# Second MLP's up projection: seven block products in place of eight

## The chip, the cores and the metric

One core of one Trainium2 chip runs one program. The metric is the device time of one execution in microseconds, the median over runs; before the change three runs gave 2939.75 us (2938.02 to 2944.45).

## What is computed

One inference step of a two-layer decoder trunk for 1024 prompt tokens and 64 sample tokens, 1088 rows in all, of width 1024. Layer 0 mixes with RWKV-7 and gated DeltaNet heads, layer 1 with an RG-LRU; each layer is followed by a squared-ReLU MLP of inner width 4096, and a final norm ends it. What the change touches is the end of layer 1:

```python
yc, hl, cl = lru_mix(xn, w_in_odd[i], lru_conv_w[i], lru_conv_b[i], ...)
h = h + yc @ w_out_odd[i]
h = h + sq_relu_mlp(rmsnorm(h, norm_mlp[l]), mlp_up[l], mlp_down[l])
y = rmsnorm(h, norm_final)

def sq_relu_mlp(x, up, down):
    return jnp.square(jax.nn.relu(x @ up)) @ down
```

## The kernel before

Activations lie transposed: `h[f]`, f = 0 to 7, is feature tile f, 128 features on the partitions and 1088 tokens along the row. Tokens come in two halves (`HALVES`): columns 0 to 575 in two chunks of 288 and columns 576 to 1087 in one chunk of 512 (`CH`). A chunk's accumulator is one PSUM bank; `dense` takes it in turn from the pools psd and psc, two banks each, so four accumulators are open at most. A third pool, psa, has two banks more.

Every large matrix product is made of three terms in float32r: an operand x is split into hi = round(x) and lo = x - hi, the weights likewise, and `dense` adds wh·xh, wh·xl and wl·xh over the tiles k of the contraction. `wraw` loads raw weights into tiles "wraw" (128 x 512, 256 KB a DMA, from SyncE's queue, SP), `wsplit` makes "whi" on ScalarE and "wlo" on VectorE. There are four raw buffers and four hi/lo pairs. `split` does the same for activations.

`lru` ends with `gate(7)`, whose product is stored to a DRAM tensor "yl", and with `rows_out`, which transposes final states and stores them from POOL's queue. `outproj` loads yl in tiles "mid" (six buffers of 576), splits them into x tiles, and adds to h the eight feature tiles of the projection, first those of half 0, then those of half 1.

`mlp(1, h)` norms h (`norm_half`: operands are split with the norm's weight, and the factor 1/rms, "rs", is applied to the product) and then runs eight blocks. In a block the up projection makes four feature tiles of the middle: 8 weight tiles x 3 terms for each of the three chunks, `relu2` takes each from PSUM, and its square is split into two "big" tiles (hi and lo; twelve buffers). The down projection then adds the block's share to all eight h[f]: 4 tiles x 3 terms for each chunk. The last block takes the chunks in turn, so that `final` can start on rows that are done.

Tile framework and engines: a scheduler puts the program's operations into one fixed order for each engine ahead of the run; each engine and each DMA queue works in that order, and what waits holds up what is behind it. A tile that reuses memory waits for the last reader of what lay there.

```python
for blk in range(8):
    for j in range(4):
        w = self.wload(up[:, :, f * P:(f + 1) * P], 8, P)
        mh, ml = self.big(F32R), self.big(F32R)
        for c0, n in chs:
            self.relu2(m, self.dense(w, 0, P, xs, c0, n), c0, n)
            self.split((mh[:, c0:c0 + n], ml[:, c0:c0 + n]), m)
```

Of the kernel before, what the change touches and what calls it, by code (L numbers as in the profile page):

```python
# [100 lines left out]
class Kern:  # L101
# [336 lines left out]
    def mlp(self, l, h, xs=None, early=0):  # L438
# [5 lines left out]
        for blk in range(8):  # L444
            mids = []
            for j in range(4):
                f = blk * 4 + j
                w = self.wload(up[:, :, f * P:(f + 1) * P], 8, P)
                mh, ml = self.big(F32R), self.big(F32R)
                chs = CH  # L450
                if f < early:
                    chs = CH[2:]
                    m = self.mid(TA)
                    nc.sync.dma_start(m, self.ma[:, f, :])
                    self.split((mh[:, :TA], ml[:, :TA]), m)
# [6 lines left out]
            passes = [(CH, ())] if blk < 7 or l == 0 else [  # L462
                (CH[:2], ()), (((TA, 256),), (0, 1, 2, 3, 8)), (((TA + 256, 256),), (4, 5)), ((), (6, 7))]
            if len(passes) > 1:
                self.final_weights()
            for chs, done in passes:
                done = list(done)
                for fo in range(4 if chs else 0):
                    w = self.wload(down[:, blk * 4:(blk + 1) * 4, fo * 256:(fo + 1) * 256], 4, 256)
                    for s in range(2):  # L470
                        f = fo * 2 + s
                        for c0, n in chs:
                            ps = self.dense(w, s * P, P, mids, c0, n)
                            self.tt(h[f][:, c0:c0 + n], h[f][:, c0:c0 + n], ps, ALU.add)
                        if f and done:
                            self.final(h, done.pop(0))
                for t in done:
                    self.final(h, t)


    def outproj(self, w_out, xs, ys, h):

        w_out = w_out.rearrange("(k p) f -> p k f", p=P)
        for hf, (c0, n, _) in enumerate(HALVES):
            for k, x in enumerate(xs):
                y = self.mid(n)
                self.nc.sync.dma_start(y[:, :512], ys[:, k, hf * 512:hf * 512 + 512])
                if hf == 0:
                    self.nc.sync.dma_start(y[:, 512:], ys[:, k, NP:])
                self.split(x[hf], y)  # L490
        for c0, n, chs in HALVES:
            for f in range(8):
                w = self.wload(w_out[:, :, f * P:(f + 1) * P], 8, P)
                for cc, m in chs:
                    ps = self.dense(w, 0, P, xs, cc, m)
                    self.tt(h[f][:, cc:cc + m], h[f][:, cc:cc + m], ps, ALU.add)


    def evac(self, pp, psx, pre, ps, c0, n, b0=0, end=NP, rs=None):
# [1118 lines left out]
def body(tc, a, o, stop=None, dbg=None):  # L1618
    with ExitStack() as es:
# [1 line left out]
        K.setup()  # L1621
        K.even()
        K.wpools(es, 4 - WBUF[0], 4 - WBUF[1])
        K.xp = K.pool(es, "xp")
        K.wk = K.pool(es, "wk")
        hp = K.pool(es, "h0")
        h = [hp.tile([P, T], F32, name=f"h{f}") for f in range(8)]
        K.dp = (K.psd, K.psc)
        for _ in K.ahead(*AHEAD[1:]):
            pass  # L1630
# [39 lines left out]
```

## Time and profile before

| what | value |
|---|---|
| runs | 2939.75 us median, 2938.02 to 2944.45 |
| the profiled execution | 2938.02 us, of it a span of 2935.6 us from first to last instruction |
| TensorE (PE) | 2843.6 us busy, 20284 matmuls |
| VectorE (DVE), ScalarE (ACT) | 1580.4 and 1131.5 us busy |
| mean granted TensorE clock | 0.984 |
| odd output projection | 2058.9 to 2155.6 us from the span's start |
| second MLP, from its first up matmul | from 2156.7 us |

Times in rows are microseconds from the span's start, unless marked ns. PE's matmuls are pipelined and their ends are modelled, so a row's duration overlaps the next row; what one costs in a stream is the distance from start to start. A wait is idle time of an engine in front of an instruction, with what ended it. An engine that waits while it is not the bottleneck costs nothing. A row of busy time by stretch holds start and end, length, then busy time and count of PE, of PE's weight loads, of DVE, ACT and POOL, then the granted clock (1.00 is 2.4 GHz), the DMA engines' busy share and the GB/s they moved.

### The profile page before, as it was taken

The page shows a single profiled execution, that of the slowest core. Times are in us where ns is not written, and L with a number is a line of the kernel's source. Part 1 is how long each engine was busy: PE and PEld are TensorE (multiplying, and loading weights), DVE is VectorE, ACT ScalarE, POOL GpSimd, SP SyncE. Part 2 cuts the span into 40 slices and gives each one's busy share as a digit, 9 for nine tenths or more (in the row PEclk, how much of TensorE's full clock was granted, in tenths as well). Part 3 has the DMA queues.
Part 4 walks back from the last instruction along what each step waited for, and adds up shares of the span by engine and source line. Part 5 has one row for each costly group of instructions (what it writes and reads, how often), then busy time and mean ns, then how long its engine had stood idle before and what let it go on. Part 6 is the DMA issues. An engine that isn't in the chain of part 4 may idle for free. (4 is left out here: it accounts for less than half of the span.)

```text
span 2935.6 us, 50667 instructions
## 1 busy us (share of the span) xinstructions
PE 2843.6 (97%) x20284; PEld 2503.9 (85%) x20284; DVE 1580.4 (54%) x3390; ACT 1131.5 (39%) x2289; POOL 126.3 (4%) x337
## 2 busy tenths in 40 slices
PE   7999998989998999999999999999999999999998
PEld 6997776667887898988889999888989999999998
DVE  4365776678747662644443336677643333333335
ACT  6455444335445432522222224656441222112224
POOL 2111001110000000000000000000000000000000
PEclk9999999799998999999999999999999999999999
DMA  5345444335344345522222111121421111111113
GB/s 187 112 120 149 115 105 106 93 98 138 108 126 125 101 139 156 176 74 81 74 78 58 44 46 44 46 67 63 150 65 44 44 44 50 44 44 44 44 58 126
DMA packets 421842, 263.21 MB, mean 90 GB/s; under 512 B 95333, under 2 KB 393119, under 8 KB 421606
## 3 DMA queue, kind: packets, MB, share of 16 engines
q1 hardware_dynamic: 415478, 243.99, 29.0%
q0 software_dynamic: 5696, 14.86, 1.6%
q8 instruction: 159, 2.61, 0.4%
q10 hardware_dynamic: 432, 1.11, 0.1%
q14 instruction: 77, 0.63, 0.1%
HBM read 206.17 MB, written 53.73 MB: 89 GB/s over the span
## 5 line engine op out<-in xcount | busy, mean ns | idle before, releaser
L157 PE MATMUL m<-xh,whi 128*128 128x288 f32 (+3 forms) x2984 | 991.3, 333 | 4.9 <-DVE big L151 1.4
L157 PE MATMUL m<-xl,whi 128*128 128x288 f32 (+3 forms) x2984 | 987.7, 331 | 0.2 <-DVE xl L151 0.2
L157 PE MATMUL m<-xh,wlo 128*128 128x288 f32 (+3 forms) x2984 | 980.4, 329 | 0.2 <-DVE wlo L151 0.2
L148 ACT ACTIVATE whi<-wraw 128x512 fp32r<-128x512 f32 x533 | 334.1, 629 | 1050.2 <-PE m L157 970.8
L157 PE MATMUL m<-big,whi 128*128 128x288 f32 (+2 forms) x3136 | 727.3, 323 | 0.0
L157 PEld LDWEIGHTS m<-xh,whi 128*128 128x128 f32 (+1 forms) x2984 | 561.6, 189 | 54.5 <-DVE big L151 2.0
L157 PEld LDWEIGHTS m<-xh,wlo 128*128 128x128 f32 (+1 forms) x2984 | 562.2, 189 | 42.8 <-issue 1.0
L157 PEld LDWEIGHTS m<-xl,whi 128*128 128x128 f32 (+1 forms) x2984 | 562.1, 188 | 42.6 <-issue 2.0
L157 PEld LDWEIGHTS m<-big,whi 128*128 128x128 f32 x3136 | 527.9, 188 | 38.1
L151 DVE TENSOR_TENSOR wlo<-wraw,whi 128x512 fp32r<-128x512 f32 x533 | 364.7, 686 | 325.3 <-ACT whi L148 316.7
L157 PE MATMUL m<-big,wlo 128*128 128x288 f32 (+2 forms) x1568 | 506.5, 323 | 0.0
L151 DVE TENSOR_TENSOR h<-h,m 128x288 f32<-128x288 f32 (+2 forms) x416 | 217.8, 524 | 353.1 <-PE m L157 353.1
L157 PEld LDWEIGHTS m<-big,wlo 128*128 128x128 f32 x1568 | 294.3, 188 | 19.4
L148 ACT ACTIVATE mid<-mid 128x288 f32<-128x288 f32 (+1 forms) x202 | 104.2, 518 | 238.9 <-DVE mid L154 203.2
L154 DVE SCALAR_TENSOR_TENSOR mid<-m,rs 128x512 f32<-128x512 f32 (+1 forms) x154 | 85.4, 554 | 176.6 <-PE m L157 176.6
L151 DVE TENSOR_TENSOR big<-mid,big 128x288 fp32r<-128x288 f32 (+2 forms) x170 | 99.4, 585 | 120.8 <-ACT big L148 120.4
L148 ACT ACTIVATE big<-mid 128x288 fp32r<-128x288 f32 (+2 forms) x170 | 92.6, 545 | 7.0 <-DMA mid<-ma 2.1
L154 DVE SCALAR_TENSOR_TENSOR fpo<-fpp,vt,fpo 128x512 f32<-128x512 f32 x100 | 74.5, 745 | 29.2 <-ACT fpo L148 24.9
L148 ACT ACT_TABLE_LOAD x62 | 79.5, 1283 | 9.4 <-PE m L157 6.3
L148 ACT ACTIVATE fpp<-m 128x288 f32<-128x288 f32 (+1 forms) x78 | 35.0, 449 | 56.2 <-PE m L157 47.8
L151 DVE TENSOR_TENSOR tbtmp<-lb,tb 32x15 f32<-32x15 f32 (+8 forms) x270 | 51.5, 191 | 6.3 <-DMA lb<-rs 2.0
L151 DVE TENSOR_TENSOR tb<-tb,tbtmp 32x15 f32<-32x15 f32 (+8 forms) x270 | 52.0, 193 | 4.6
(386 smaller groups left out, 2580.2 us busy)
## 6 DMA issues: line engine op xcount, KB each, us to landing
wraw<-mlp_up SPq DMA_DIRECT2D x172, 256.0 KB
wraw<-mlp_down SPq DMA_DIRECT2D x144, 256.0 KB
wraw<-w_in_even SPq DMA_DIRECT2D x120, 256.0 KB
wraw<-w_out_even SPq DMA_DIRECT2D x32, 256.0 KB
wraw<-w_in_odd SPq DMA_DIRECT2D x32, 256.0 KB
wraw<-w_out_odd SPq DMA_DIRECT2D x32, 256.0 KB
in<-rd SPq DMA_DIRECT2D x8, 896.0 KB
mid<-ma SPq DMA_DIRECT2D x22, 288.0 KB
```

Source lines behind the costliest of these rows:

```text
L148: return self.nc.scalar.activation(out, in_, f, **kw)
L151: return self.nc.vector.tensor_tensor(out, a, b, op)
L154: return self.nc.vector.scalar_tensor_tensor(out, a, s, b, op0, op1, **kw)
L157: return self.nc.tensor.matmul(out, l, r, start=start, stop=stop, **kw)
```

## The change

The up projection of the second MLP is made by Strassen's scheme (Winograd's form). A pair j of feature tiles (2j, 2j+1), the two halves of the contraction (h[0..3] and h[4..7]) and a pair of token chunks (288 and 288, or 256 and 256) give 2 x 2 blocks, and the four block results come from seven block products in place of eight. Each product adds over four tiles k. Its operands are sums of blocks: of weights, made for each pair ("s1", "s2" and one raw tile overwritten), and of the normed h ("T1" to "T4", and three plain blocks), made once and kept for all 16 pairs in new pools (xq: 2 x 28 operands as hi and lo). The 512 chunk of half 1 is now a pair of 256. Three banks a pair of chunks (A, B, C) hold the products; B takes three in turn, read out between by DVE into temporaries "t1", "u2", "u3".

The operands are computed while the output projection runs. Its loads from yl now go through four buffers "tx" of 288 columns, and its feature tiles come in the order 0, 4, 1, 5, 2, 6, 3, 7. The finished middle is stored to DRAM ("mb") by SP, chunk by chunk, and only when all of it is made are the pools of the operands given back and the pool with "mid" and "big" opened again: `mlp_down` then runs the eight down blocks one behind the other, loading each middle tile and splitting it. The down projection itself, with its order at the end, is as it was.

```diff
+    def mlp_down(self, l, h, mb):
+        down = self.a["mlp_down"][l].rearrange("(k p) f -> p k f", p=P)
+        for blk in range(8):
+            mids = []
+            for j in range(4):
+                mh, ml = self.big(F32R), self.big(F32R)
+                for c0, n, _ in HALVES:
+                    m = self.mid(n)
+                    self.nc.sync.dma_start(m, mb[:, blk * 4 + j, c0:c0 + n])
+                    self.split((mh[:, c0:c0 + n], ml[:, c0:c0 + n]), m)
...
+    def up_fast(self, es, l, h, mb, w_out, ys):
...
+        tmp = lambda n, tag="tx", bufs=4: tp.tile([P, 288], F32, name=tag, bufs=bufs)[:, :n]
+        pair = lambda i: xq.tile([P, 512], F32R, name=f"xs{i}", bufs=1)
+        pairs = [((0, 288), (288, 288)), ((TA, 256), (TA + 256, 256))]
...
+        for k in range(8):
+            for o in (0, 288):
+                y = tmp(288)
+                if o:
+                    nc.sync.dma_start(y[:, :224], ys[:, k, 288:512])
+                    nc.sync.dma_start(y[:, 224:], ys[:, k, NP:])
+                else:
+                    nc.sync.dma_start(y, ys[:, k, :288])
+                self.split([x[:, o:o + 288] for x in xa[k]], y)
...
+        def operands(half, ks):
...
+            for name in ("B11", "T2", "B21", "T3", "T1", "T4", "B22"):
+                for k in ks:
+                    if name == "B11":
+                        x = part(src(k, a0), w(k))
+                    elif name == "T2":
+                        t2[k] = tmp(n, "t2", 2)
+                        self.tt(t2[k], src(k, b0), src(k, a0), ALU.subtract)
+                        self.act(t2[k], t2[k], AF.Copy, scale=w(k))
+                        self.stt(t2[k], src(k + 4, b0), w(k + 4), t2[k], ALU.mult, ALU.subtract)
+                        x = part(t2[k])
...
+        for hf, (c0, n, chs) in enumerate(HALVES):
+            for i, f in enumerate((0, 4, 1, 5, 2, 6, 3, 7)):
                 w = self.wload(w_out[:, :, f * P:(f + 1) * P], 8, P)
                 for cc, m in chs:
                     ps = self.dense(w, 0, P, xs, cc, m)
                     self.tt(h[f][:, cc:cc + m], h[f][:, cc:cc + m], ps, ALU.add)
+                if hf:
+                    steps(first, 6)
+                    if i > 4:
+                        steps(second, 4)
...
+        def weights(j):
+            r11, r12 = self.wraw(up[:, :, 2 * j * P:(2 * j + 1) * P], 8, P)
+            r21, r22 = self.wraw(up[:, :, (2 * j + 1) * P:(2 * j + 2) * P], 8, P)
+            s1, s2 = [sp.tile([P, 512], F32, name="sw", bufs=2) for _ in range(2)]
+            yield self.wsplit([r11], P)
+            self.tt(s1, r21, r22, ALU.add)
+            self.tt(s2, s1, r11, ALU.subtract)
+            yield self.wsplit([s2], P)
+            yield self.wsplit([r12], P)
+            self.tt(r21, r11, r21, ALU.subtract)
+            yield self.wsplit([r21], P)
+            self.tt(s2, r12, s2, ALU.subtract)
+            yield self.wsplit([s1], P)
+            yield self.wsplit([r22], P)
+            yield self.wsplit([s2], P)
+
+        def out(f, x, src, c0, n):
+            self.stt(x, src, 0.0, self.r(c0, n), ALU.max, ALU.mult)
+            self.act(x, x, AF.Square)
+            nc.sync.dma_start(mb[:, f, c0:c0 + n], x)
+
+        def product(j, w, i, half):
+            name, b, start = (("B11", "A", 1), ("T2", "B", 1), ("B21", "A", 0), ("T3", "B", 0), ("T1", "C", 1),
+                              ("T4", "B", 0), ("B22", "C", 0))[i]
...
+            if name == "B11":
+                q["t1"] = tmp(n, "t1", 2)
+                self.act(q["t1"], ps)
+            elif name == "T2":
+                q["u2"] = tmp(n, "u2", 2)
+                self.tt(q["u2"], ps, q["t1"], ALU.add)
+            elif name == "B21":
+                out(2 * j, tmp(n), ps, a0, n)
+            elif name == "T3":
+                q["u3"] = tmp(n, "u3", 2)
+                self.tt(q["u3"], ps, q["t1"], ALU.add)
+            else:
+                x = tmp(n)
+                self.tt(x, ps, q[{"T1": "u3", "T4": "t1", "B22": "u2"}[name]], ALU.add)
...
+                out(2 * j + f, x, x, c0, n)
...
+        for j in range(1, 16):
+            for i, w in enumerate(weights(j)):
+                for half in range(2):
+                    product(j, w, i, half)
...
-        K.outproj(a["w_out_odd"][0], K.xtiles(), ys, h)
-        K.mlp(1, h)
+        main.close()
+        mb = K.dr.tile([P, 32, T], F32, name="mb")
+        with ExitStack() as fast:
+            K.up_fast(fast, 1, h, mb, a["w_out_odd"][0], ys)
+        K.wk = K.pool(es, "wk")
+        K.mlp_down(1, h, mb)
```

The order on three places. First SP's queue between the LRU and the output projection, before ("yl" is the LRU's result in DRAM, "mid" a load buffer; the store is that of the last of eight tiles):

```order
L250 DMA wraw<-w_out_odd 128x4x128
L487 DMA mid<-yl 128x512
L489 DMA mid<-yl 128x64
L487 DMA mid<-yl 128x512
L489 DMA mid<-yl 128x64
L487 DMA mid<-yl 128x512
L489 DMA mid<-yl 128x64
L487 DMA mid<-yl 128x512
L489 DMA mid<-yl 128x64
L487 DMA mid<-yl 128x512
L630 DMA yl<-big 128x1088
```

and of the change:

```order
L250 DMA wraw<-w_out_odd 128x4x128 x2
L841 DMA yl<-big 128x1088
L524 DMA tx<-yl 128x288
L521 DMA tx<-yl 128x224
L522 DMA tx<-yl 128x64
L524 DMA tx<-yl 128x288
L521 DMA tx<-yl 128x224
L522 DMA tx<-yl 128x64
```

The four and a half loads that stood ahead of the last store now stand behind it, and there are three for each tile of yl instead of two. Next DVE in a pair of feature tiles of the up projection, of the change ("sw" are the sums of weights, "u" and "t" the temporaries, "tx" a result on its way out):

```order
L151 TENSOR_TENSOR wlo<-sw,whi 128x512
L151 TENSOR_TENSOR sw<-wraw 128x512
L151 TENSOR_TENSOR u_24641<-m,t_24535 128x288
L151 TENSOR_TENSOR sw<-sw,wraw 128x512
L151 TENSOR_TENSOR wraw<-wraw 128x512
L151 TENSOR_TENSOR u_24655<-m,t_24550 128x256
L151 TENSOR_TENSOR wlo<-wraw,whi 128x512
L151 TENSOR_TENSOR tx<-m,u_24641 128x288
```

The sum of the next pair's raw weights (second row) stands ahead of the two evictions of the fourth product (third and sixth row). Last SP's queue from the up to the down projection, of the change:

```order
L655 DMA mb<-tx 128x288
L655 DMA mb<-tx 128x256
L250 DMA wraw<-mlp_down 128x2x256
L655 DMA mb<-tx 128x288
L489 DMA mid<-mb 128x576
L655 DMA mb<-tx 128x256
L489 DMA mid<-mb 128x512
```

The first load of the middle stands behind the last store but one, and the other loads behind the last. There was no such load before.

## Rows read from the trace of the kernel before

**Rows 1.** The page: busy time by engine, and granted clock in 40 slices.

```profile
PE 2843.6 (97%) x20284; PEld 2503.9 (85%) x20284; DVE 1580.4 (54%) x3390; ACT 1131.5 (39%) x2289; POOL 126.3 (4%) x337
...
PEclk9999999799998999999999999999999999999999
```

**Rows 2.** PE's waits from 2060 to 2900 us: total, times, longest.

```profile
PE m L157 <- DVE xl L151: 0.2, 1, 0.2
```

**Rows 3.** PE in order of time, second MLP: start, us, instruction, count.

```profile
2172.16 0.29 PE L157 MATMUL m<-xh,whi 128*128 128x288 f32 x1
...
2178.53 0.40 PE L157 MATMUL m<-xh,whi 128*128 128x512 f32 x1
...
2184.01 0.29 PE L157 MATMUL m<-xh,whi 128*128 128x288 f32 x1
...
2895.62 0.28 PE L157 MATMUL m<-big,whi 128*128 128x256 f32 x1
...
2898.50 0.27 PE L160 MATMUL m<-ct,h 128*128 128x128 f32 x1
```

**Rows 4.** Busy time in one stretch: length, then engines, clock, DMA share, GB/s.

```profile
2219.50:2267.00 47.50, 47.50 (x291) 43.63 (x290) 17.28 (x31) 7.05 (x13) 0.00 (x0) 1.00 0.16 47
```

**Rows 5.** PE in order of time, LRU to output projection.

```profile
2053.66 1.03 PE L160 MATMUL m<-ct,lcvo 128*27 128x128 f32 x8
...
2058.94 1.06 PE L157 MATMUL m<-xh,whi 128*128 128x288 f32 x4 [1.23 <-ACT xh L148]
...
2060.58 0.44 PE L157 MATMUL m<-xh,wlo 128*128 128x288 f32 x1
2060.82 0.44 PE L157 MATMUL m<-xh,whi 128*128 128x288 f32 x1
...
2064.05 0.29 PE L157 MATMUL m<-xh,wlo 128*128 128x288 f32 x1
...
2073.79 0.30 PE L157 MATMUL m<-xh,whi 128*128 128x288 f32 x1
```

**Rows 6.** SP's queue in order of time, the same place.

```profile
2054.02 0.58 SPq L487 DMA_DIRECT2D mid<-yl  x1
...
2057.49 0.43 SPq L489 DMA_DIRECT2D mid<-yl  x1
...
2060.75 0.32 SPq L630 DMA_DIRECT2D yl<-big  x1
```

**Rows 7.** The chain that ended last, the same place: start, us, what.

```profile
2054.66 2.32 DMA mid<-yl
```

**Rows 8.** Busy time by stretches of 2 us, the same place.

```profile
2060.00:2062.00 2.00, 1.83 (x8) 1.83 (x8) 2.00 (x5) 1.36 (x2) 0.54 (x2) 0.50 0.77 232
...
2066.00:2068.00 2.00, 2.00 (x17) 2.00 (x16) 2.00 (x3) 1.34 (x3) 0.00 (x0) 1.00 0.99 357
```

**Rows 9.** DVE by line, 2172 to 2850: count, busy us, mean ns.

```profile
L151 DVE TENSOR_TENSOR wlo<-wraw,whi 128x512 fp32r<-128x512 f32 x115 | 79.1, 688 | 75.4 <-ACT whi L148 74.1 <-PE m L157 1.4
...
L154 DVE SCALAR_TENSOR_TENSOR mid<-m,rs 128x288 f32<-128x288 f32 x59 | 27.0, 457 | 60.3 <-PE m L157 60.3
```

**Rows 10.** ACT by line and shape, 2172 to 2850.

```profile
L148 ACT ACTIVATE whi<-wraw 128x512 fp32r<-128x512 f32 x115 | 72.7, 632 | 379.1 <-PE m L157 363.9 <-DVE wlo L151 15.3
...
L148 ACT ACTIVATE mid<-mid 128x288 f32<-128x288 f32 x58 | 25.8, 444 | 124.8 <-DVE mid L154 124.8
```

**Rows 11.** POOL's stores of the LRU state: when issued, time to landing.

```profile
L536 POOL DMA_DIRECT2D out_lru_s<-big x2: 502/507/512, 2059.1 to 2060.0; - x2
...
DMA to landing us min/median/max: 2.4/2.6/2.7
```

**Rows 12.** ACT in order of time, LRU to output projection.

```profile
2061.32 0.69 ACT L148 ACTIVATE xh<-mid 128x576 fp32r<-128x576 f32 x1 [0.29 <-DMA mid<-yl]
```

**Rows 13.** DVE in order of time, two of 288 columns in a row.

```profile
2050.00 0.45 DVE L151 TENSOR_TENSOR mid<-m,rs 128x288 f32<-128x288 f32 x1
2050.37 0.45 DVE L151 TENSOR_TENSOR mid<-mid 128x288 f32<-128x288 f32 x1
```

More of the change, by code (lines that the diff above doesn't have):

```diff
@@ L460, in mlp @@
                 mids.append([(mh[:, :TA], ml[:, :TA]), (mh[:, TA:], ml[:, TA:])])
-            passes = [(CH, ())] if blk < 7 or l == 0 else [
-                (CH[:2], ()), (((TA, 256),), (0, 1, 2, 3, 8)), (((TA + 256, 256),), (4, 5)), ((), (6, 7))]
-            if len(passes) > 1:
-                self.final_weights()
[L466 to L478, printed above, removed]
@@ L481, in outproj @@
-    def outproj(self, w_out, xs, ys, h):
-        w_out = w_out.rearrange("(k p) f -> p k f", p=P)
[L484 to L492, printed above, removed]
+            self.down_block(down, blk, mids, h)
@@ new lines, in down_block @@
+    def down_block(self, down, blk, mids, h, passes=((CH, ()),)):
+        for chs, done in passes:
+            done = list(done)
+            for fo in range(4 if chs else 0):
+                w = self.wload(down[:, blk * 4:(blk + 1) * 4, fo * 256:(fo + 1) * 256], 4, 256)
+                for s in range(2):
+                    f = fo * 2 + s
+                    for c0, n in chs:
+                        ps = self.dense(w, s * P, P, mids, c0, n)
+                        self.tt(h[f][:, c0:c0 + n], h[f][:, c0:c0 + n], ps, ALU.add)
+                    if f and done:
+                        self.final(h, done.pop(0))
+            for t in done:
+                self.final(h, t)
@@ L496, in outproj @@
                     self.tt(h[f][:, cc:cc + m], h[f][:, cc:cc + m], ps, ALU.add)
+                if hf:
+                    steps(first, 6)
+                    if i > 4:
+                        steps(second, 4)
+        self.rs = [self.rtile(0), tp.tile([P, 512], F32, name="rsq", bufs=1)]
+        fac = chain(factors(0), factors(1))
+        def weights(j):
[13 more added lines that the diff above has]
+            yield self.wsplit([s2], P)
@@ new lines, in up_fast @@
+        steps(first, 28)
+        ws = {}
+        for i, w in enumerate(chain(weights(0), (None, None))):
+            ws[i] = w
+            if i == 0:
+                steps(fac, 2)
+            steps(second, 4)
+            if w:
+                product(0, w, i, 0)
+            if i == 4:
+                steps(fac, 2)
+            if i > 1:
+                product(0, ws[i - 2], i - 2, 1)
+        for j in range(1, 16):
+            for i, w in enumerate(weights(j)):
+                for half in range(2):
+                    product(j, w, i, half)
@@ L1623, in body @@
         K.wpools(es, 4 - WBUF[0], 4 - WBUF[1])
-        K.xp = K.pool(es, "xp")
-        K.wk = K.pool(es, "wk")
         hp = K.pool(es, "h0")
         h = [hp.tile([P, T], F32, name=f"h{f}") for f in range(8)]
+        main = ExitStack()
+        K.xp = K.pool(main, "xp")
+        K.wk = K.pool(main, "wk")
         K.dp = (K.psd, K.psc)
```

104 lines of the change are left out of this document (added).

## The prediction

> **What bounds the kernel now.** I read the page first: the share of each engine and the 40 slices [rows 1]. TensorE (PE) is busy for 97% of the span with its clock granted almost throughout, VectorE (DVE) for 54%, ScalarE (ACT) for 39%. Busy PE can hide gaps, since ends are modelled, so the second view is the list of PE's waits from 2060 us on [rows 2]: one wait of 0.2 us up to 2900 us. From the odd output projection to the last blocks PE is fed without a break, and only its own pace counts there. That pace is the third view, start to start in the timeline [rows 3]: 48 matmuls of 288 columns from 2172.16 to 2178.53, so 132.7 ns each; 24 of 512 columns from there to 2184.01, 228.3 ns; 24 of 256 from 2895.62 to 2898.50, 120.0 ns. A column is not the whole price: about 20 to 30 ns stand on every matmul, so cutting 512 into two halves costs. A stretch of the second MLP [rows 4] shows what room the others have: in 47.5 us DVE worked 17.3 and ACT 7.1. The last views are on the one place near the change where PE does starve, between the LRU and the output projection [rows 5 to 8].
>
> **The change part by part.**
>
> *Products instead of the up projection.* Removed: 32 feature tiles x 8 weight tiles x 3 terms = 768 matmuls for each of the chunks 288, 288, 512: 768 x (2 x 132.7 + 228.3) = 379.2 us [rows 3]. Added: 16 pairs x 7 products x 4 x 3 = 1344 matmuls of 288 and 1344 of 256 columns: 1344 x (132.7 + 120.0) = 339.6 us. Gain **39.5 us**. If a matmul of 256 were no cheaper than one of 288, the gain would be 22; I take 120.0, since the 24 ran unbroken. The Trainium skill ("TensorE: Matmul & The Clock Gate", Back-to-back issue gap) puts a matmul at its columns over 2.4 GHz plus 2.5 ns; by that estimate the gain would be 42.5 us, but the trace is 10 to 13 ns above it at each of the three widths.
>
> *DVE and ACT inside a pair.* One pair holds PE for 84 x 252.7 ns = 21.2 us. DVE has 29 instructions in it: 7 weight splits and 4 sums of 512 columns at 0.69, and 18 of 288 or 256 at no more than 0.46 [rows 9]: 15.9 us. ACT has 7 splits at 0.63 and 10 instructions of 0.45 [rows 10]: 8.9 us. Both are below PE, and the middle's own splits, which the old form made here, move to the down stage. So this costs PE nothing on average; order can still hurt (first rival). Bank reuse: a product's bank is written again three half-products or more later, over 4.5 us, against an eviction of 0.46. I take 1 us for all steady pairs, bounds 0 and 8.
>
> *Seam from LRU to output projection.* Before, the first load of the projection's operand left at 2054.02, ahead of the last 544 KB store, which left at 2060.75 [rows 6]; PE started on it at 2058.94, after a lean stretch since 2053.66, opened four banks, 96 matmuls, and was through with them at 2073.79 [rows 5]. In the new order all loads stand behind that store, and its first two buffers lie where the last LRU tiles were, which POOL's last stores still read: one issued at 2059.1 with 2.7 us to landing, one at 2060.0 with 2.4 [rows 11]. So the first tile leaves at about 2061.8 and the second at 2062.4. There are 16 tiles in four buffers, that is four rounds. A round is a load of 2.95 (issued 2054.02, landed 2056.97 [rows 6, 7]; a later one, issued 2057.49, was there at 2061.32, 3.8 on [rows 6, 12]), an ACT and a DVE split of 0.45 each [rows 9, 10], and some 0.9 for issuing, since half of the tiles take two DMAs of 0.43 [rows 6]: 4.8 us. The last split ends at 2061.8 + 4 x 4.8 = 2081, and the four banks at 2082.6 after the last 12 matmuls: 8.8 us late. Behind that, the weights' second half waits on DVE for two of the later tiles, about 2 us. I take **+10.8**; bounds 4.2 (rounds keep up with PE, which only starts 6 us later, less what it waited before) and 18 (3.8 us a load and the clock low).
>
> *Operands beside the projection.* In the second half of the projection (8 x 24 x 228 ns = 43.8 us) DVE has 8 adds and 16 weight splits at 0.69 and some 55 operand and norm instructions that follow each other every 0.37 [rows 9, 13]: 37 us. It fits. In the first pair DVE still owes half of the second half's operands and both norm factors: some 25 us of work against 21.2 of PE. The old norm put the same kind of work there under no PE wait [rows 2], since it needed only one split a tile. Walking the new order, PE stands before the factor matmuls and once or twice at a bank: **+2.5**, bounds 0 and 8.
>
> *Seam from up to down.* Before there was none: the middle came out of PSUM. Now PE ends its last half-product at a time 0. The store ahead of the first load waits for the half before it, which ended 1.44 us earlier, and for two DVE instructions, an ACT square and the issue: the load leaves at +0.3, lands at +3.2, is split by ACT at +3.9 (576 columns, 0.69 [rows 12]) and PE starts. The next loads stand behind the last store, at +1.7, and the fourth tile's waits for a buffer that DVE frees at 4.7; it is split at +9.8. PE's four open banks are 7.5 us of work, 1.9 of it on the fourth tile, so they end at 11.7: 4.2 late. The clock adds to it: after the hole of 2054 to 2059 it was granted at 0.50 (1.2 GHz) for 2060 to 2062 [rows 8], and 24 matmuls took 2058.94 to 2064.05 [rows 5], 5.1 us where 24 x 132.7 ns make 3.2. That is 1.9. The next block's splits stand before two adds, 1.4. I take **+7.5**; bounds 3 and 14.
>
> *Seams between down blocks.* Twelve "big" buffers, eight in use, so two tiles of each block are split only while the block before ends. The last 512 group takes 2.7 us and frees them in turn; two ACT and three DVE steps later the fourth is there at about +1.0 to +1.4, and PE reaches it at +1.2. Seven times 0.15: **+1**, bounds 0 and 6. The down stage's DMAs grow by 2.2 MB a block of 47 us, to some 90 GB/s; [rows 8] show 232 and 357. The end, with its norm, is unchanged.
>
> Sum: -39.5 + 1 + 10.8 + 2.5 + 7.5 + 1 = **-16.7 us**. Against the profiled execution (2938.0 us, of it 2935.6 span) this is 2921.3; it lies 1.7 below the median of the runs, so I forecast **2923 us**.
>
> **The rivals.**
>
> *DVE stands behind a weight on its way* (slower). A raw weight buffer is freed only when its split is made. In each pair the last raw tile of the next pair can be asked for at 7.6 us (second product done 6.1, ACT 0.63, DVE 0.69, issue), lands L later, and DVE's sum of it stands in its queue ahead of the eviction that PE needs before its sixth product, at 15.2 us. It holds while L is below 6.4 us. Beyond, each further us is paid 15 times: at L = 7.5 the gain is gone, at 9 the kernel takes 2962. For it: 8 stores a pair share SP's queue, and each waits for ACT. Against it: the same kind of load took 2.95 to 3.8 us here, at higher rates [rows 6 to 8, 12].
>
> *The clock stays low through both seams.* PE is fed in small pieces for 20 us at the first and 10 at the second. At the half clock a 288-column matmul came every 0.24 us, from 2060.58 to 2060.82 [rows 5]. Then 96 of them need 23 us from 2065.1, not 2082.6 but 2088, and the second seam ends at 18 and not 11.7: +12 in all, **2935**. The Trainium skill ("TensorE: Matmul & The Clock Gate", Loop structure matters more than you think) says that DMA waits between bursts leave PE cold. The trace agrees as far as its one hole goes; but there the remaining 72 matmuls came at 135 ns, with the loads still under way, which speaks against.
>
> *The seams are nearly free.* Rounds keep pace with PE, the waits of the first pair vanish: 4.2 + 4 + 1 + 0 in place of 22.8, **2910**.
>
> **How the numbers follow.** The forecast's case, 2914 to 2931, gets 0.64: the gain is counted, the seams are bounded by rows. Free seams 0.12, low clock 0.14, DVE behind a weight 0.10. The range that leaves out 2 in 10 is 2911 to 2937: it cuts the slower rival, the upper end of the clock's and the lowest part of the free seams. A measurement can tell 0.2%, 5.9 us, from no change: faster is below 2933.9. Forecast and free seams are faster whole, of the clock's 0.04: 0.80. Within 0.2%: 0.10 of the clock's and 0.02 of the slower rival: 0.12. Slower: 0.08.
>
> **What would show it.** Right: pairs 21.2 us apart, with PE never over 0.5 us idle in one; the first operand split of the projection near 2065 and the four banks done near 2083; 4 us of PE idle where up turns into down. Wrong: DVE idle on a raw weight's DMA in every pair and PE behind it (first rival); granted clock 0.5 over more than 5 us at a seam (second); 256-wide matmuls at more than 127 ns apart, which would be a mis-sized gain; or waits of over 1 us at each of the seven down seams, which I priced at next to nothing.

## The result and the profile after

The changed kernel takes **2917.5 us** (median of 6 runs, 2912.2 to 2919.1) against 2939.4 for the kernel before (now 6 runs, 2938.0 to 2944.7): a ratio of 0.9918, interval 0.9905 to 0.9931. The profiled execution of the changed kernel took 2916.9 us with a span of 2914.8; against the one of before (2938.0, span 2935.6) the span is 20.8 us shorter where the sum said 16.7.

The page of the changed kernel, busy time by engine and granted clock, answers to [rows 1].

```profile
PE 2811.8 (96%) x20670; PEld 2500.4 (86%) x20670; DVE 1736.0 (60%) x3775; ACT 1184.5 (41%) x2461; POOL 126.9 (4%) x337
...
PEclk9999998889998999999999999999999999999999
```

PE works 32 us less, DVE 156 us more. DVE's larger share costs nothing by itself: that is seen in PE's waits from 2045 to 2900 us (total, times, longest), where [rows 2] had 0.2 us after 2060.

```profile
PE m L157 <- ACT xh L148: 7.9, 2, 7.7
PE m L157 <- ACT big L148: 4.8, 3, 4.1
PE m L160 <- DVE big L745: 1.8, 2, 1.0
PE m L157 <- DVE rsq L151: 0.2, 1, 0.2
```

So there are two holes, and none in the pairs of products. The third row is the recurrence's own wait; the kernel before has the same 1.8 us there. The pace of the pairs stands in the timeline of PE; [rows 3] are its rows of before.

```profile
2174.29 0.30 PE L157 MATMUL m<-xeh,whi 128*128 128x288 f32 x1
...
2175.89 0.40 PE L157 MATMUL m<-xs,whi 128*128 128x256 f32 x2
...
2177.31 0.30 PE L157 MATMUL m<-xeh,whi 128*128 128x288 f32 x1
```

Twelve matmuls of 288 columns take 1.60 us (133 ns each), twelve of 256 take 1.42 (118 ns). A pair is 7 x (1.60 + 1.42) = 21.1 us.

**Where the time went.** The next table cuts each profiled execution at the starts of PE's matmuls. A is the recurrence's last one; the stretches that follow add up to the end of the span, to within 0.1 us. PE's work ahead of A is the same in every kernel of this study, but for a few neighbouring matmuls that change places, yet A lies anywhere from 2050 to 2067 us, so single times and medians carry a spread that the change has no part in. The stretch from A to the end doesn't carry it, and most verdicts below rest on that.

| us | before | after | difference | the prediction's term |
|---|---|---|---|---|
| A | 2057.44 | 2058.70 | +1.3 | none |
| A to the projection's first matmul | 1.50 | 7.96 | +6.5 | with the next row +10.8 |
| projection, first half | 53.08 | 54.57 | +1.5 | |
| projection, second half | 43.56 | 43.56 | 0 | 0 |
| up projection (before: norm 4.7 + 8 x 47.39) | 383.8 | 343.7 | -40.1 | -39.5 + 1 + 2.5 |
| up to down, PE idle | 0 | 4.2 | +4.2 | with the next row +7.5 |
| first down block (the others: 47.25) | 47.25 | 52.21 | +5.0 | |
| down blocks 2 to 7, each | 47.25 | 47.25 | 0 | +1 in all |
| down block 8, to the last matmul | 56.56 | 56.57 | 0 | 0 |
| behind the last matmul | 8.85 | 9.81 | +1.0 | 0 |

**The first seam**, SP's queue in the changed kernel, in order of time (start, us, engine, line, operation, what it moves); [rows 6] are those of before.

```profile
2061.93 0.35 SPq L841 DMA_DIRECT2D yl<-big  x1
2062.38 0.38 SPq L524 DMA_DIRECT2D tx<-yl  x1
2064.12 0.32 SPq L521 DMA_DIRECT2D tx<-yl  x1
```

The first operand load leaves 3.7 us after A, where before it left 3.4 us ahead of it. It follows the store at once, so its place behind the store is what held it last; the second load waits 1.3 us more for memory that one of POOL's last stores still reads (SP's list of waits, 2050 to 2075):

```profile
SPq L521 <- DMA out_lru_s<-big: 1.3, 1, 1.3
```

ACT's rows show the splits of the first, the fifth, the ninth and the thirteenth of the sixteen tiles, and a weight split between; the bracket is ACT's idle time and what ended it.

```profile
2066.16 0.97 ACT L148 ACTIVATE xh<-tx 128x288 fp32r<-128x288 f32 x2 [6.59 <-DMA tx<-yl]
...
2069.22 0.44 ACT L148 ACTIVATE xh<-tx 128x288 fp32r<-128x288 f32 x1 [0.67 <-DMA tx<-yl]
...
2072.30 0.45 ACT L148 ACTIVATE xh<-tx 128x288 fp32r<-128x288 f32 x1 [0.17 <-DMA tx<-yl]
2074.27 0.63 ACT L148 ACTIVATE whi<-wraw 128x512 fp32r<-128x512 f32 x1 [1.52 <-PE m L157]
...
2077.45 0.44 ACT L148 ACTIVATE xh<-tx 128x288 fp32r<-128x288 f32 x1 [0.30 <-DMA tx<-yl]
```

The first two rounds of four buffers take 3.1 us each, not the 4.8 that I had priced; the third takes 5.2, with ACT standing 1.5 us in front of a weight split that waits for PE. The granted clock by stretches of 2 us (length, PE, PEld, DVE, ACT, POOL, clock, DMA share, GB/s) answers to [rows 8]: it is 0.50 (1.2 GHz) while PE gets its first matmuls, up to 2070, and 1.00 in the stretch from 2072 on.

```profile
2066.00:2068.00 2.00, 1.34 (x5) 1.35 (x6) 0.93 (x3) 1.33 (x3) 0.00 (x0) 0.50 0.57 153
...
2070.00:2072.00 2.00, 2.00 (x14) 2.00 (x13) 1.07 (x3) 1.20 (x3) 0.00 (x0) 0.77 0.68 192
2072.00:2074.00 2.00, 2.00 (x17) 2.00 (x16) 0.92 (x2) 0.57 (x2) 0.00 (x0) 1.00 0.68 174
```

**The second seam.** The last product's last matmul starts at 2508.34. SP issues one load of the middle ahead of the last store, and seven behind it:

```profile
2509.22 0.32 SPq L489 DMA_DIRECT2D mid<-mb  x1
2510.06 0.32 SPq L655 DMA_DIRECT2D mb<-tx  x1
2510.48 5.82 SPq L489 DMA_DIRECT2D mid<-mb  x7
```

ACT's rows of the same place: the first split waits 1.9 us for that load, the second as long again.

```profile
2509.62 0.42 ACT L148 ACTIVATE tx<-tx 128x256 f32<-128x256 f32 x1 [0.41 <-ACT whi L148]
2511.96 0.68 ACT L148 ACTIVATE big<-mid 128x576 fp32r<-128x576 f32 x1 [1.92 <-DMA mid<-mb]
2514.59 0.63 ACT L148 ACTIVATE big<-mid 128x512 fp32r<-128x512 f32 x1 [1.95 <-DMA mid<-mb]
```

### The profile page after: what moved, and what is told of

It reads as the page before. It is cut to its first block, busy times and chain, and to the rows that moved or that the text cites. A ratio compares the mean times of both kernels' runs of the same rounds, so it can differ in the third digit from the quotient of the medians.

```text
span 2914.8 us, 52681 instructions
## 1 busy us (share of the span) xinstructions
PE 2811.8 (96%) x20670; PEld 2500.4 (86%) x20670; DVE 1736.0 (60%) x3775; ACT 1184.5 (41%) x2461; POOL 126.9 (4%) x337
## 5 line engine op out<-in xcount | busy, mean ns | idle before, releaser
L157 PE MATMUL m<-xh,whi 128*128 128x288 f32 (+4 forms) x2408 | 791.5, 330 | 11.5 <-ACT xh L148 7.9
L157 PE MATMUL m<-xl,whi 128*128 128x288 f32 (+4 forms) x2408 | 787.0, 327 | 0.0
L157 PE MATMUL m<-xh,wlo 128*128 128x288 f32 (+4 forms) x2408 | 780.4, 325 | 0.3 <-DVE wlo L151 0.3
L157 PEld LDWEIGHTS m<-xh,whi 128*128 128x128 f32 (+1 forms) x2408 | 453.7, 189 | 49.3 <-ACT xh L148 9.2
L157 PEld LDWEIGHTS m<-xl,whi 128*128 128x128 f32 (+1 forms) x2408 | 454.2, 189 | 29.9 <-issue 2.0
L157 PEld LDWEIGHTS m<-xh,wlo 128*128 128x128 f32 (+1 forms) x2408 | 453.7, 189 | 30.0 <-issue 1.0
L157 PE MATMUL m<-xs,whi 128*128 128x256 f32 (+1 forms) x1024 | 204.6, 295 | 0.0
L157 PEld LDWEIGHTS m<-xs,whi 128*128 128x128 f32 x1024 | 163.2, 189 | 5.1
L157 PE MATMUL m<-xs,wlo 128*128 128x256 f32 (+1 forms) x512 | 151.1, 295 | 0.0
L157 PEld LDWEIGHTS m<-xs,wlo 128*128 128x128 f32 x512 | 97.0, 189 | 2.5
```

The costliest lines, as they stand in the source:

```text
L157: return self.nc.tensor.matmul(out, l, r, start=start, stop=stop, **kw)
```

## The experiments

What the kernels gave by the same cuts (hole: from the last product's last matmul to the first down matmul, start to start; in the kernel that keeps the clock, with the added matmuls in it; first down block: up to the start of the second, with any wait ahead of that):

| us | A | A to projection | first half | up | hole | first down block | A to end | median of the runs |
|---|---|---|---|---|---|---|---|---|
| before | 2057.44 | 1.50 | 53.08 | | | 47.25 | 878.1 | 2939.4 |
| after | 2058.70 | 7.96 | 54.57 | 343.6 | 4.36 | 52.21 | 856.1 | 2917.5 |
| loads first | 2056.00 | 1.50 | 53.94 | 343.5 | 4.32 | 51.54 | 847.5 | 2906.6 |
| more buffers | 2054.41 | 8.16 | 54.13 | 343.6 | 4.65 | 51.59 | 855.0 | 2914.5 |
| GpSimd's queue | 2066.62 | 8.19 | 54.46 | 343.6 | 2.33 | 49.68 | 852.1 | 2916.4 |
| clock kept | 2055.38 | 8.05 | 54.45 | 343.6 | 4.58 | 51.44 | 855.6 | 2911.8 |
| apart | 2059.05 | 1.50 | 54.12 | 383.6 | 3.72 | 50.00 | 885.4 | 2943.0 |
| both | 2050.47 | 1.50 | 53.45 | 343.5 | 2.32 | 50.61 | 844.1 | 2907.9 |
| early block | 2055.80 | 7.95 | 55.05 | 346.5 | 0.12 | 57.02 | 862.4 | 2925.3 |
| early, loads first | 2058.92 | 1.28 | 53.67 | 346.5 | 0.12 | 56.81 | 854.3 | 2911.5 |
| kept block | 2060.64 | 1.50 | 53.50 | 346.5 | 0.12 | 49.38 | 843.6 | 2905.2 |
| slots | 2063.46 | 1.50 | 53.39 | 346.5 | 4.73 | 51.21 | 850.0 | 2914.3 |

Three things bound what this table can tell. The medians of different rows can't be set against each other as they are: the kernel before, run beside each group, had 2939.4 us beside the changed kernel, 2940.6 beside the four from "loads first" to "clock kept", 2938.0 beside the four from "apart" to "early, loads first", 2941.3 beside "kept block" and 2945.6 beside "slots". Stretches that no edit touched spread too: the first half is 54.45 to 55.05 us in four kernels with the same code there, 53.08 and 54.12 in the two with the old code; hole and first block together are 55.9 to 56.6 us in the four that leave that seam as the change made it. And the stretch behind the last matmul is 9.8 us in the changed kernel, "GpSimd's queue" and "clock kept", 9.1 in "more buffers" and 8.85 in all others; why stays open.

### The first half's loads in their old place

```
+        xa = K.xhalf(K.xpb, TA)
+        for k in range(8):
+            y = K.mid(TA)
+            tc.nc.sync.dma_start(y[:, :512], ys[:, k, :512])
+            tc.nc.sync.dma_start(y[:, 512:], ys[:, k, NP:])
+            K.split(xa[k], y)
         main.close()
...
-        for k in range(8):
-            for o in (0, 288):
-                y = tmp(288)
...
```

> The changed kernel, with the eight operand loads of the projection's first half and their splits made as the kernel before makes them: 576 columns at a time, through the six buffers named mid, and ahead of the return of the recurrence's memory. The pairs of products and the seam into the down projection are untouched. Theory 1 (the loads start late, since their buffers are new memory that the recurrence gives back only with its last stores): PE's first wait of the projection goes from 11.7 us back towards the 5.3 of the kernel before, the stretch to the end of half 0 from 66.3 to 58 to 60 us, the time 6 to 8 us under the changed kernel, 2909.5 to 2911.5. Theory 2 (the start is the same, and rounds of four half-width loads cost the time): the wait stays above 10 us, the 96 matmuls go from 16.3 to 14.9 us, the time 1 to 2 us lower, 2915.5 to 2916.5. Theory 3 (the seam is set by the last state stores, whatever reads them): no change, 2917.5.

Measured: 2906.6 us (ratio to before 0.9890, 0.9872 to 0.9908), 8.6 us less from A to the end; 7.1 of the 8.6 stand at this seam, 0.7 at the second and 1.0 behind the last matmul, which the edit doesn't touch. Counted as in the expectation, from the first of the eight matmuls that start 3.8 us ahead of A, the wait is 5.3 us for 11.7 and the stretch to the end of half 0 59.2 for 66.3. SP's queue shows the first load back ahead of A (2056.00) and of the last store:

```profile
2052.61 0.58 SPq L1845 DMA_DIRECT2D mid<-yl  x1
...
2059.31 0.32 SPq L831 DMA_DIRECT2D yl<-big  x1
```

and PE's list of waits has the wait of before:

```profile
PE m L157 <- ACT big L148: 4.6, 2, 4.0
...
PE m L157 <- ACT xh L148: 1.2, 1, 1.2
```

Of the 7.95 us that the first seam cost, 7.1 are gone, and with the spread of the first half nothing is left that could be told from zero. Theory 1 holds: what the seam costs is the late start of the loads.

### More buffers for the loads

```
-                y = tmp(288)
+                y = tmp(288, *more[(2 * k + o // 288 + 4) % 10])
```

> The changed kernel, with the sixteen loads of the projection's first half turning over ten buffers of 288 columns for four; they stay half-width and behind the return of the recurrence's memory. Theory 1 (late start): the first wait stays at 11 to 12 us and only the rounds' share, at most the 1.5 us by which the 96 matmuls were longer, comes back: 2916 to 2917.5. Theory 2 (rounds of four): 4 us or more come back, 2913.5 or less.

Measured: 1.1 us less from A to the end, 2914.5 us (2911.5 to 2914.7), between the numbers of the two theories. With ten buffers the loads follow each other without a round, but the first still leaves behind the last store:

```profile
2057.65 0.35 SPq L842 DMA_DIRECT2D yl<-big  x1
2058.09 0.38 SPq L525 DMA_DIRECT2D t<-yl  x1
```

and PE's first wait, of 7.9 us, is untouched:

```profile
PE m L157 <- ACT xh L148: 7.9, 1, 7.9
```

Counted as in the expectation that is 11.9 us. So rounds, by which I had reckoned the term, cost at most some 0.4 us (first half 54.57 to 54.13), and the same code gave 54.45 to 55.05. Theory 2 falls.

### The first block's loads on GpSimd

```
-                    self.nc.sync.dma_start(m, mb[:, blk * 4 + j, c0:c0 + n])
+                    (self.nc.sync if blk else self.nc.gpsimd).dma_start(m, mb[:, blk * 4 + j, c0:c0 + n])
```

> The changed kernel, with the eight loads of the first down block's middle values issued by GpSimd for SyncE; all stores of the middle stay on SyncE. Theory 1 (the loads stand behind the last stores of the middle on SyncE, which wait for the last adds): the loads are issued before the last product ends, PE's wait ahead of the down projection goes from 4.1 us to under 1, the first down block from 52.2 towards 47.3 us as the clock stays up, the time 5 to 9 us under the changed kernel, 2908.5 to 2912.5. Theory 2 (the wait is for the data itself, or for memory that the last pair holds): the wait stays above 3 us, and the time within 1.5 us of 2917.5.

Measured: 4.0 us less from A to the end, with A 7.9 us later than in the profiled execution of the changed kernel, so the median (2916.4, 2906.7 to 2920.6) shows next to nothing of it. Hole and first block take 52.0 us for 56.6. Six of the loads left between 2502.9 and 2510.3, up to 13 us ahead of the last product's end,

```profile
2502.92 0.58 POOL L489 DMA_DIRECT2D mid<-mb  x1 [433.19 <-DVE wlo L151]
...
2508.69 1.60 POOL L489 DMA_DIRECT2D mid<-mb  x3 [3.77 <-PE m L157]
```

and PE's wait fell to 2.0 us, not under 1. What is left is ACT's order: all six splits stand behind the last eviction of the products, and run without a wait.

```profile
2517.66 0.42 ACT L148 ACTIVATE tx<-tx 128x256 f32<-128x256 f32 x1 [0.21 <-ACT whi L148]
2517.98 3.39 ACT L148 ACTIVATE big<-mid 128x576 fp32r<-128x576 f32 x6
```

Theory 1 gave the mechanism but not all of its size.

### PE kept busy through the hole

The kernel does 32 matmuls that the reference doesn't ask for.

```
+                if fo == 0 and blk == 0 and not self.kept:
+                    self.kept = True
+                    ps = self.bank(self.psb)
+                    for _ in range(32):
+                        self.mm(ps[:, :256], w[0][0][:, :P], w[0][0])
```

> The changed kernel with added work: 32 matmuls of 256 columns on the first down weight, whose result nobody reads, stand between the last product and the first down matmul, about 32 x 0.118 = 3.8 us in a hole of 4.1 us. Theory 1 (of the 9.2 us of this seam, some 2 to 4 are the half-rate clock behind the hole): the granted clock stays near 1 from 2508 to 2520, the first down block is 48 to 50 us for 52.2, the time 2 to 4 us lower, 2913.5 to 2915.5. Theory 2 (only the arrival of the loads and their splits counts): the clock is higher, and the time within 1 us of 2917.5, or over it by what the added matmuls overrun.

Measured: the granted clock is 1.00 through the seam, by stretches of 4 us,

```profile
2512.00:2516.00 4.00, 3.71 (x22) 3.25 (x23) 3.52 (x6) 3.49 (x6) 0.00 (x0) 1.00 0.90 300
2516.00:2520.00 4.00, 2.66 (x16) 1.99 (x14) 1.23 (x2) 0.63 (x1) 0.00 (x0) 1.00 0.94 296
```

where the changed kernel had

```profile
2512.00:2516.00 4.00, 2.85 (x8) 2.01 (x8) 1.45 (x2) 1.65 (x3) 0.00 (x0) 0.50 0.97 277
2516.00:2520.00 4.00, 3.72 (x13) 3.41 (x13) 3.46 (x5) 3.27 (x6) 0.00 (x0) 0.50 0.93 297
```

and still hole and first block take 56.0 us for 56.6. The added matmuls hold nothing up: the first down matmul behind them still waits 0.46 us for ACT. PE runs ahead at full clock and then stands (its waits inside the first block are 2.6 us for 0.7): ACT, whose splits it needs, waits for the loads, which move at 296 GB/s.

```profile
2518.73 0.63 ACT L149 ACTIVATE big<-mid 128x512 fp32r<-128x512 f32 x1 [2.90 <-DMA mid<-mb]
```

By these cuts theory 2 holds; the median, 2911.8 us (2906.8 to 2914.9), lies under the numbers of both theories, but only 0.5 us of that stand behind A. The half clock of this seam is there, but it is not what the seam costs: its share is some 0.6 us by these two kernels, which is within the spread of the seams left untouched (55.9 to 56.6).

### The middle through DRAM, without the seven products

```
-        K.mlp(1, h)
+        K.mlp_apart(1, h)
+    def mlp_apart(self, l, h):
...
+        for f in range(32):
+            w = self.wload(up[:, :, f * P:(f + 1) * P], 8, P)
+            for c0, n in CH:
+                m = self.mid(n)
+                self.relu2(m, self.dense(w, 0, P, xs, c0, n), c0, n)
+                nc.sync.dma_start(mb[:, f, c0:c0 + n], m)
+        for blk in range(8):
...
```

> The kernel before, with the second MLP's up projection run whole ahead of its down projection and the middle stored to and loaded from DRAM, as the changed kernel does; the up projection keeps its eight block products, and the seam behind the recurrence is the old one. Theory 1 (the seam up to down is the price of the middle through DRAM, whatever products stand ahead of it): PE waits 4 to 5 us ahead of the down projection, the first down block is 51 to 53 us long, and the time is 8 to 10 us over the kernel before, 2947 to 2951; the products' own gain is then the difference from here to the run with the operand loads first, some 40 us. Theory 2 (the seam comes of the half-width stores and the adds ahead of them): the wait is under 2 us and the time within 3 us of the kernel before.

Measured: 2943.0 us (11 runs) against 2938.0 (17 runs), a ratio of 1.0022 (1.0009 to 1.0035), that is 2.6 to 10.3 us slower; from A to the end 7.3 us more. PE's wait at the seam:

```profile
PE m L157 <- ACT big L148: 3.3, 1, 3.3
```

Hole and first block cost 3.6 + 2.75 = 6.4 us here, 9.2 in the changed kernel. So some two thirds of that seam belong to the middle through DRAM whatever stands ahead of it (theory 1, a little under its numbers); the other 2.8 (2.1 to 2.8 by the four untouched seams) appear only with the changed kernel's form of the up stage; which part of it holds them was not tried. And the products alone: the up stage takes 383.6 us here and 343.6 in the changed kernel, 40 us less.

### Both edits together

```
+            tc.nc.sync.dma_start(y[:, :512], ys[:, k, :512])
...
+                    (self.nc.sync if blk else self.nc.gpsimd).dma_start(m, mb[:, blk * 4 + j, c0:c0 + n])
```

> The changed kernel with both earlier edits, the operand loads of the projection's first half ahead of the return of the recurrence's memory and the first down block's loads on GpSimd. From the recurrence's last matmul to the end the changed kernel's profiled execution took 856.1 us, 847.5 with the first edit and 852.1 with the second. Theory 1 (two separate seams, which add up): 843 to 844.5 us, and the time 2901 to 2904. Theory 2 (the second edit's gain was the spread of the code ahead of it, not its own): 846.5 to 848.5 us, and the time about 2906.

Measured: 844.1 us from A to the end, inside theory 1's numbers, and by the table 7.6 us less at the first seam and 3.6 at the second, 1.0 behind the last matmul: the seams add up. The median, 2907.9 us (2896.4 to 2909.3; ratio 0.9892, 0.9873 to 0.9910), is not below that of the first edit alone; five runs that spread over 13 us can't show 3.5.

### The first down block made during the last pair

```
+                for x, y in self.xhalf(self.xpb, TA):
+                    for o in (0, 288):
+                        yield x[:, o:o + 288], y[:, o:o + 288]
                 for i in range(12):
                     yield [xq.tile([P, 288], F32R, name=f"xe{p}{i}", bufs=1) for p in "hl"]
...
+                if j == 15 and i:
+                    early(i)
+        down = self.a["mlp_down"][l].rearrange("(k p) f -> p k f", p=P)
+        self.down_block(down, 0, list(zip(*mids)), h)
...
+                    nc.sync.dma_start(mids[i - 1][q][1].bitcast(F32), mb[:, q, c0:c0 + n])
```

> The changed kernel, with the first down block's middle loaded and split during the last pair of products, into memory whose operands that pair has already used; the seam behind the recurrence is untouched. Theory 1 (arrival and the splits' place in ScalarE's order make the whole 9 us of this seam; PE's clock only follows): PE's wait ahead of the down projection is under 1 us, the first down block 47.3 to 48.5 us for 52.2, the stretch from the recurrence's last matmul to the end 846.5 to 849 us for 856.1, the time 2907.5 to 2910.5. Theory 2 (VectorE and ScalarE are full in the pairs, so eight more splits there hold up the last products by what they save behind them): the last pair is 4 us or more longer than 21.1, and the stretch over 852 us.

Measured: slower, 2925.3 us (2915.6 to 2929.0), 862.4 from A to the end, 6.3 more than the changed kernel. Neither theory: the last pair is 21.2 us, not 4 longer, but two waits took the place of one. The edit does a second thing as well, which the expectation doesn't name: its first lines move the operands of the pairs to other slots. The up stage is 346.5 us for 343.6, so 3.0 of the 6.3 us come with that (the last experiment has it alone). PE's waits from 2480 to 2580 us:

```profile
PE m L157 <- ACT big L148: 4.7, 2, 4.2
PE m L157 <- ACT xh L148: 3.2, 1, 3.2
```

The second is inside the first block, behind its ninth matmul (a load that SP issued at 2507.3, between stores and weights). The first is a new one, ahead of the *second* block: the pool that it uses is opened only behind the first block's instructions, and SP's loads for it leave some 46 us later, behind all of the first block's weights.

```profile
2515.86 46.16 SPq L250 DMA_DIRECT2D wraw<-mlp_down  x8
2562.12 5.69 SPq L489 DMA_DIRECT2D mid<-mb  x8
```

### The same, with the first seam closed

This is the kernel above with the loads first as well.

```
+            tc.nc.sync.dma_start(y[:, :512], ys[:, k, :512])
...
+                if j == 15 and i:
+                    early(i)
```

> Both seams closed: the operand loads of the projection's first half ahead of the return of the recurrence's memory, and the first down block's middle loaded and split during the last pair. Theory 1 (the seams add up): from the recurrence's last matmul to the end 838 to 841 us for the 856.1 of the changed kernel, and the time 2895 to 2900. Theory 2 (the earlier block gains nothing): 846.5 to 848.5 us and about 2906.

Measured: 2911.5 us (2907.0 to 2916.2), 854.3 from A to the end, 8.0 less than the kernel above and 6.8 more than the loads first alone. Neither theory: the second seam is worse than untouched. Hole and the first two blocks take 107.5 us for 103.1 in the loads first alone, and the other slots cost 3.0 in the up stage.

### The first block in memory that stays

```
+                for x, y in self.xhalf(self.xpb, TA):
+                    for o in (0, 288):
+                        yield x[:, o:o + 288], y[:, o:o + 288]
                 for i in range(12):
                     yield [xq.tile([P, 288], F32R, name=f"xe{p}{i}", bufs=1) for p in "hl"]
...
+                    hl = [self.xpb.tile([P, TA], F32R, name=f"x{p}{q + 2 * i - 2}")[:, :n] for p in "hl"]
+                    nc.gpsimd.dma_start(hl[1].bitcast(F32), mb[:, q, c0:c0 + n])
```

> The run that closed both seams, with two things mended: the first down block's middle lies in memory that no pool gives back (the slots of the projection's first operands, which the first four operands of the pairs now use), so that nothing of the second block waits for it, and its loads are issued by GpSimd, free of the stores and weights in SyncE's order. Theory 1 (what the earlier block lost was the second block's loads, issued behind all weights of the first, and loads late by SyncE's order): no wait of over 1 us ahead of the second down block, under 1.5 us ahead of the first, the first block 47.3 to 49 us, from the recurrence's last matmul to the end 838 to 841 us, the time 2896 to 2900. Theory 2 (VectorE and ScalarE, full in the pairs, hold the last pair up by as much): the wait ahead of the first block is still over 2 us or the last pair over 24 us, and the stretch 843 us or more.

Measured: 2905.2 us (2896.9 to 2910.8; ratio 0.9882, 0.9860 to 0.9905). PE's waits from 2480 to 2580 us are one:

```profile
PE m L157 <- ACT xh L148: 1.3, 1, 1.3
```

The hole is gone, the first block is 49.4 us, nothing stands ahead of the second. Yet the stretch from A is 843.6 us for the 838 to 841 expected: the up stage had grown by 3.0 us, by a wait in the first pair and by pairs of 21.21 us for 21.13. Theory 1's waits came and its stretch didn't; theory 2's stretch came, but neither of its signs, since the wait is under 2 us and the last pair 21.2. The kernels with the early block had the same 346.5 us in the up stage.

### The exchange of slots alone

The edit is the exchange of slots shown in the section before, on top of the loads first.

> The run with the operand loads first, and of the last run only the exchange of slots: the first sixteen operands of the first half go to the slots of the projection's operands, the last twelve to new memory; the first down block is loaded and split as in the changed kernel. The last run's pairs were 21.21 us apart for 21.13, with a wait of 1.6 us in the first pair. Theory 1 (both come of the exchange of slots, and took back 3 us of what the earlier first block gained): pairs 21.2 us apart, the 1.6 us wait is there, and from the recurrence's last matmul to the end 850 to 851 us for 847.5. Theory 2 (they come of the loads and splits put into the last pair): pairs 21.13 us, no such wait, 847 to 848 us.

Measured: pairs of 21.21 us, up stage 346.5, from A to the end 850.0, and the wait:

```profile
PE m L157 <- DVE tx L154: 1.6, 1, 1.6
```

Theory 1: the 3 us come of the exchange of slots, not of the work put into the last pair. Why a pair is 0.08 us longer when the same operands lie in other slots stays open.

## Why the prediction was right

The time lies in the range, 5.5 us under the forecast, and by the step that carried it: the gain of the products, less what the two seams cost. The single terms were off by 1 to 3 us each, most of them too dear.

- **The products** (-39.5, with +1 for the steady pairs): -41.1, since 16 pairs of 21.13 are 338.0 us where the eight old blocks took 379.1. The prices from [rows 3] were right to 2 ns: 133 and 118 measured for 132.7 and 120.0. (The prediction's "20 to 30 ns on every matmul" doesn't come out of those rows: from 288 to 512 columns they rise by 0.43 ns a column, which leaves some 10 ns. No term used it.) The kernel with the up stage apart shows the gain alone, 40 us with the norm and the first pair. The estimate from the Trainium skill ("TensorE: Matmul & The Clock Gate", Back-to-back issue gap) was 42.5: as far off as the term from the rows, though by that rule a pair would be 19.5 us. The Trainium skill gives this rule for a matmul by itself and says that in a stream it counts too much at 512 columns; the trace shows the opposite, 228.3 ns there [rows 3] for the rule's 215.8. The estimate came out all the same because its error, 25 us on the old up projection and 27 on the new, nearly falls out of the difference.
- **DVE inside a pair** was right to cost nothing: DVE's share rose to 60%, and PE's list has no wait on it beyond 0.2 us from the first pair on. The slower rival, DVE behind a weight's DMA, didn't come.
- **The seam at the recurrence** (+10.8): +7.95, the largest miss. The late start was right: PE's first matmul came 8.0 us after A, where the prediction's 2065.1 lies 7.7 after. What was mis-sized is what stands behind it. "Four rounds at 4.8 us" were taken to be PE's path, with the four banks done 25.2 us after A. The last split did come about when forecast (23.9 us after A for 23.6), but PE hardly waited for it: behind its first matmul it stood 0.2 us, the banks were done 24.3 after A, and ten buffers, with the last split 1.9 us earlier, gave back 0.2 of that. "The weights' second half, about 2 us" was nothing: from the four banks to the end of the first half all kernels take 38.2 to 38.3 us.

  What the prediction put first, loads behind the last store and memory that POOL still reads, is the cause: with the old loads in their old place 7.1 of the 7.95 are gone. That run moved place, memory and width together; the changed kernel's queue shows the place for the first load and 1.3 us of memory for the second, but how much each holds alone was not tried. The sign named, four banks done near 2083, came true (2083.0) by two errors that cancelled: they were 0.9 us less behind A than forecast, and A was 1.3 us later.
- **Operands and first pair** (+2.5): about +1.
- **The seam up to down** (+7.5): +9.2. PE's idle time was as named, 4.1 us. But "the clock adds 1.9" was the wrong term: with the clock kept at full the seam is 0.6 us shorter, no more than untouched seams differ. What the runs show in its place is the wait for loads and splits: loads sent earlier took 4.6 us off hole and block together (2.9 with the loads first in both kernels), and with the splits made earlier too they are 49.5 us for 55.9.
- **Between down blocks** (+1): 0, six blocks of 47.25 us.
- **Not in the sum:** 1.3 us ahead of A and 1.0 behind the last matmul, which no step of the change touches; seven of the ten later kernels don't have the 1.0.

The sign that I had named for the low clock, 0.50 over more than 5 us at a seam, did appear (2062 to 2070 and 2512 to 2520), without the 12 us that I had tied to it. The Trainium skill ("TensorE: Matmul & The Clock Gate", Loop structure matters more than you think) says that DMA waits between bursts leave PE cold, and it was; but at the second seam a cold PE that would have waited for its operands anyway lost no more than some 0.6 us by it. A sign should have been the wait, not the clock.

The best kernels of the study are the loads in their old place, alone or with either remedy of the second seam: 2906.6, 2907.9 and 2905.2 us. From A to the end the last two are 3.4 and 3.9 us shorter than the first, which the spread ahead of A hides in the medians. By their ratios to the kernel before, 0.9890, 0.9892 and 0.9882 for the 0.9918 of the changed kernel, they beat it by 8 to 11 us; from A to the end by 8.6 to 12.5.

## What to carry to other kernels

Price a new form of the matmuls from rows of the same width, and look for the loss at its two ends: what was gained in the products followed from their number and price to 2 us (and hung, by 3, on the slots of their operands), while what is lost depends on which queue, which memory and which place in an engine's order the first loads and splits behind the seam have. Before blaming a low clock at a hole, ask whether the operands would have been there sooner; added matmuls that keep the clock up answer that in one run. And when work is drawn ahead of a seam, ask whose memory it holds: the next block's loads may wait for that instead.

## What the runs showed of the hardware

The same code ahead of A took 2050.5 to 2066.6 us in twelve profiled executions, more than half of what the change is worth; the runs of the kernel before alone spread from 2929.3 to 2949.8 us. Part of this is seen in the granted clock between 400 and 600 us, here in the changed kernel and in the one with the loads first:

```profile
400.00:600.00 200.00, 180.32 (x1599) 130.02 (x1599) 134.86 (x373) 86.04 (x216) 22.14 (x48) 0.86 0.39 99
```

```profile
400.00:600.00 200.00, 177.68 (x1627) 129.01 (x1623) 136.27 (x376) 88.11 (x222) 22.12 (x48) 0.90 0.39 101
```

A cut at a fixed matmul takes this out of a comparison; a median of five runs does not. The other surprise is the 0.08 us that a pair of 168 matmuls gained or lost with the slots of its operands (21.13 or 21.21), the same to the second decimal in 13 pairs in a row of each kernel: 21.13 in all six with the old slots, 21.21 in all four with the slots exchanged. Of the 0.08 us 0.05 stand on the matmuls of 256 columns, whose operands the edit doesn't name; why stays open.
